# Warm-up matmuls of TensorE 512 columns wide in place of 128, in an RMS norm and QKV projection

## Chip, cores, metric

One core of a Trainium2 chip. The metric is the device time of one execution in microseconds. A run's time is some 1.8 us longer than the span of its profile, which goes from the first instruction to the last. Engines: PE is TensorE's matmul side, PEld its weight loads, DVE is VectorE, ACT is ScalarE, POOL is GpSimd, SP is SyncE, which here issues nearly all DMAs, strictly in program order.

## The reference

```python
batch, n_heads, seq, head_dim = 8, 12, 1024, 64      # dim = 768
rms = np.sqrt(np.mean(x ** 2, axis=-1, keepdims=True) + eps)
x_norm = x / rms * gamma
return np.matmul(x_norm, w_qkv)                       # 8192 x 768 times 768 x 2304, f32
```

## The kernel before

x is 64 tiles of 128 rows. Each tile is cast to bf16, transposed (tiles 0 to 2 by fp32 transposes on PE, tile 3 by bf16 ones, from tile 4 on by DMA, the helper `xbar`), multiplied with the bf16 weights into PSUM, scaled by 1/rms on the way out and stored. Gamma is folded into the weights when they are converted. The first 44 us, the head, follow a hand-made plan, in which weights arrive in 12 pieces. PE is kept busy with matmuls of zeros from the start, so that its clock is fast when data comes.

```python
warm = singles.tile([P, P], bf16)                 # P = 128, NT = 512
nc.vector.memset(warm, 0.0)
# ... (cut)
def idle(n):
    wps = psum.tile([P, P], f32, name="pm")
    for _ in range(n):
        nc.tensor.matmul(out=wps, lhsT=warm, rhs=warm, start=True, stop=True)
# ... (cut)
at(0.0, idle, 18)
at(2.8, gamma_in)                                 # one small transpose and a copy
at(2.81, idle, 28)
# ... (cut; the plan of the head has idle(3) at 7.26)
for t in range(HEAD, MT):                         # HEAD = 6, MT = 64
    ahead = 6.0 if t < HEAD + 5 else 0.0          # tiles 6 to 10 are prepared 6 us earlier
    if ("x", t) not in {q[1:] for q in LOADS}:
        at(now - 15 - ahead, load_x, t)
    at(now - 8.5 - ahead, cast, t)
    at(now - 7.5 - ahead, xbar, t)
    # ... (cut: statistics, 5 x 6 matmuls, evictions, stores)
```

## Time and profile before

| | before |
|---|---|
| time, median of 3 runs | 389.1 us (388.9 to 389.16) |
| span | 387.3 us |
| PE busy | 99% of the span |
| bytes moved by DMA | 119.91 MB, 310 GB/s on average |

PE is busy by this table from end to end. What it does not say is what PE waits for in the few places where it waits. The prediction shows those lines.

### The profile page before, as it was taken

How to read it: one execution, taken by the hardware profiler on the slowest of the kernel's cores; microseconds unless marked ns; L12 is line 12 of the kernel's file. 1: busy time of each engine (PE TensorE's matmuls, PEld its weight loads, DVE VectorE, ACT ScalarE, POOL GpSimd, SP SyncE). 2: the span in 40 equal slices, each digit the busy share in tenths (PEclk: the TensorE clock that was granted, in tenths of full speed). 3: DMA queues.
4: the chain of work that ended last, by engine and by line, in shares of the span. 5: the costliest groups of instructions: out<-in, count | busy, mean ns of one | idle time of the engine just before them, and what ended most of it. 6: DMA issues, size and time to landing. Idle time of an engine off the chain costs nothing.

```text
span 387.3 us, 5554 instructions
## 1 busy us (share of the span) xinstructions
PE 381.7 (99%) x1994; PEld 194.7 (50%) x1994; DVE 153.9 (40%) x309; ACT 181.2 (47%) x362; POOL 7.5 (2%) x15
## 2 busy tenths in 40 slices
PE   8999999999999999999999999999999999999996
PEld 7444654554554554554554554554554554554552
DVE  3565524444333344333344333343333343333332
ACT  5662444443544444544444444544444534444532
POOL 0312000000000000000000000000000000000000
PEclk9999999999999999999999999999999999999999
DMA  8999999999999999999999999999999999999974
GB/s 287 390 273 389 330 361 353 372 365 323 306 289 303 311 298 317 300 297 319 292 303 303 290 328 300 296 314 292 303 274 327 322 313 287 278 352 284 307 253 182
DMA packets 89511, 119.91 MB, mean 310 GB/s; under 512 B 52358, under 2 KB 61324, under 8 KB 89484
## 3 DMA queue, kind: packets, MB, share of 16 engines
q1 hardware_dynamic: 89472, 119.56, 101.1%
q8 instruction: 15, 0.25, 0.3%
q14 instruction: 12, 0.10, 0.1%
q10 hardware_dynamic: 12, 0.00, 0.0%
HBM read 32.25 MB, written 75.50 MB: 278 GB/s over the span
## 4 chain that ended last, share of the span: by engine, by line
PE 94%; DMA 4%; POOL 0%; SPq 0%; ACT 0%; issue 0%
PE pm L229 94%; DMA w_f<-in_w_qkv_dram 3%; DMA x_t<-in_x_dram 1%; POOL w_b L168 0%; ACT ot L245 0%; SPq L158 0%; SPq L153 0%
## 5 line engine op out<-in xcount | busy, mean ns | idle before, releaser
L229 PE MATMUL pm<-w_b,xT 128*128 128x512 bf16 (+1 forms) x1920 | 374.1, 358 | 0.5 <-DVE w_b L164 0.4
L229 PEld LDWEIGHTS <-xT 128*128 128x128 bf16 x1920 | 187.7, 98 | 186.4 <-issue 1.3
L243 DVE TENSOR_SCALAR ot<-pm,rstd 128x512 f32<-128x512 f32 (+1 forms) x165 | 113.6, 693 | 201.8 <-PE pm L229 201.5
L245 ACT ACTIVATE ot<-pm,rstd 128x512 f32<-128x512 f32 (+1 forms) x155 | 100.2, 647 | 191.5 <-PE pm L229 146.6
L183 ACT ACTIVATE sq<-x_t 128x768 bf16<-128x768 f32 x64 | 53.4, 835 | 1.3 <-DMA x_t<-in_x_dram 1.2
L172 DVE CAST xb<-x_t 128x768 bf16<-128x768 f32 x61 | 33.3, 546 | 16.7 <-DMA x_t<-in_x_dram 16.7
L185 ACT ACTIVATE rms<-ssq,eps_sb 128x1 f32<-128x1 f32 x64 | 18.9, 295 | 2.1
L183 ACT ACTIVATION_READ_ACCUMULATOR sq<-x_t 128x1 f32 x64 | 12.3, 192 | 0.0
L190 DVE RECIPROCAL rstd<-rms 128x1 f32<-128x1 f32 x64 | 9.8, 154 | 3.1 <-ACT rms L185 3.1
L166 ACT ACTIVATE w_b<-w_f,g_sb 128x512 bf16<-128x512 f32 (+1 forms) x9 | 5.8, 668 | 6.1 <-DMA w_f<-in_w_qkv_dram 6.1
L168 POOL TENSOR_SCALAR w_b<-w_f,g_sb 128x512 bf16<-128x512 f32 (+1 forms) x9 | 6.8, 764 | 24.1 <-DMA w_f<-in_w_qkv_dram 24.1
L164 DVE TENSOR_SCALAR w_b<-w_f,g_sb 128x512 bf16<-128x512 f32 (+1 forms) x12 | 5.2, 450 | 4.5 <-DMA w_f<-in_w_qkv_dram 4.4
L278 PE MATMUL pm<-warm 128*128 128x128 bf16 x49 | 5.2, 294 | 1.0 <-DVE eps_sb L137 1.0
L278 PEld LDWEIGHTS <-warm 128*128 128x128 bf16 x49 | 4.7, 138 | 1.0 <-DVE eps_sb L137 1.0
L210 PE MATMUL pm<-ident_f,x_t 128*128 128x128 f32 x18 | 2.5, 278 | 0.3 <-DMA x_t<-in_x_dram 0.3
L210 PEld LDWEIGHTS pm<-ident_f,x_t 128*128 128x128 f32 x18 | 1.9, 141 | 0.7 <-PE pm L278 0.5
L172 DVE CAST xT<-pm 128x512 bf16<-128x512 f32 (+1 forms) x3 | 1.8, 592 | 0.8 <-PE pm L210 0.8
L140 ACT ACT_TABLE_LOAD x1 | 1.3, 1283 | 1.3 <-PEq L334 1.3
L174 ACT CAST xT<-pm 128x256 bf16<-128x256 f32 (+1 forms) x3 | 1.2, 445 | 0.3 <-PE pm L210 0.2
L174 ACT COPY xT<-pm 128x768 bf16<-128x768 bf16 x1 | 0.8, 798 | 0.2 <-PE pm L196 0.2
L261 DVE COPY g_sb<-pm 128x6 f32<-128x6 f32 x1 | 0.2, 164 | 1.8 <-PE pm L260 1.8
L196 PEld LDWEIGHTS <-xb 128*128 128x128 bf16 x6 | 0.4, 98 | 0.2
(13 smaller groups left out, 2.4 us busy)
## 6 DMA issues: line engine op xcount, KB each, us to landing
out_dram<-ot SPq DMA_DIRECT2D x124, 512.0 KB, 3.9
x_t<-in_x_dram SPq DMA_DIRECT2D x64, 384.0 KB, 4.3
out_dram<-ot SPq DMA_DIRECT2D x64, 128.0 KB, 3.2
w_f<-in_w_qkv_dram SPq DMA_DIRECT2D x7, 768.0 KB, 8.1
out_dram<-ot SPq DMA_DIRECT2D x8, 256.0 KB, 2.0
w_f<-in_w_qkv_dram SPq DMA_DIRECT2D x4, 256.0 KB, 6.1
xT<-xb SPq DMA_TRANSPOSE x60, 4.4
w_f<-in_w_qkv_dram SPq DMA_DIRECT2D x1, 512.0 KB, 3.9
```

The costliest lines, as they stand in the source:

```text
L164: nc.vector.tensor_scalar(out=o, in0=i, scalar1=g, scalar2=None, op0=mult)
L166: nc.scalar.activation(out=o, in_=i, func=AF.Copy, scale=g, bias=0.0)
L168: nc.gpsimd.tensor_scalar(out=o, in0=i, scalar1=g, scalar2=1.0, op0=mult, op1=mult)
L172: nc.vector.tensor_copy(out=out, in_=in_)
L183: nc.scalar.activation(out=sq, in_=X[t], func=AF.Square, accum_out=ssq)
L185: nc.scalar.activation(out=rms, in_=ssq, func=AF.Sqrt, scale=inv_k, bias=eps_sb)
L190: nc.vector.reciprocal(out=r, in_=RS[t])
L210: nc.tensor.transpose(out=PT[t, h][:, ko - k0, :], in_=X[t][:, ko * P:(ko + 1) * P], identity=ident_f)
L229: nc.tensor.matmul(out=PM[t, n0][:, :nl], lhsT=XT[t][:, ko, :], rhs=w_b[:, ko, n0:n0 + nl], start=(b == 1), stop=(b == KO))
L243: nc.vector.tensor_scalar(out=o, in0=pm[:, :nl], scalar1=RS[t], scalar2=None, op0=mult)
L245: nc.scalar.activation(out=o, in_=pm[:, :nl], func=AF.Copy, scale=RS[t], bias=0.0)
L278: nc.tensor.matmul(out=wps, lhsT=warm, rhs=warm, start=True, stop=True)
```

## The change

Its intent is the same warm-up time with a fourth of the instructions: one matmul of 512 columns for four of 128.

```diff
-    warm = singles.tile([P, P], bf16)
+    warm = singles.tile([P, NT], bf16)
...
-    def idle(n):
-        wps = psum.tile([P, P], f32, name="pm")
+    def idle(n, nl=P):
+        wps = psum.tile([P, NT], f32, name="pm")
         for _ in range(n):
-            nc.tensor.matmul(out=wps, lhsT=warm, rhs=warm, start=True, stop=True)
+            nc.tensor.matmul(out=wps[:, :nl], lhsT=warm[:, :P], rhs=warm[:, :nl], start=True, stop=True)
...
-    at(0.0, idle, 18)
+    at(0.0, idle, 4, NT)
     at(2.8, gamma_in)
-    at(2.81, idle, 28)
+    at(2.81, idle, 6, NT)
+    at(2.82, idle, 3)
```

## The prediction

> **What bounds the kernel now.** I read four views in this order: the chain of work that ended last, TensorE's (PE's) row of waits, PE's timeline over the first 22 us, and the instructions of the warm-up line.
>
> The chain of the kernel before, in order of time (start us, length us, what):
>
> ```profile
> 1.75 4.86 DMA x_t<-in_x_dram
> ...
> 6.62 10.19 DMA w_f<-in_w_qkv_dram
> ...
> 16.90 0.99 POOL w_b L168
> ...
> 17.94 365.63 PE pm L229 x1883
> ...
> 383.59 0.47 ACT ot L245
> ```
>
> The end is set by three things in a row: input transfers until 16.82 us, one weight conversion on POOL, and then 365.63 us in which PE runs without a hole. The warm-up line (L278 of the kernel before) is nowhere in it. The last part is at the array's pace: the head's twelve 512-wide matmuls from 8.70 us span 2.75 us with a last one of 379 ns, so 11 intervals of 215.6 ns; the 1883 of the chain are 1499 of 512 columns (64 tiles x 24 = 1536, less the 37 issued before 17.94 us) and 384 of 256 columns. 1499 x 0.2156 + 384 x about 0.109 (my estimate: half, plus a little) = 365.0 us, against 365.63. Nothing is left to win there, and the warm-up, over by 8 us, cannot act there unless it leaves the array at a slow clock.
>
> PE's own waits over the whole kernel (who waited, for whom, us in total, times, longest):
>
> ```profile
> PE pm L278 <- DVE eps_sb L137: 1.0, 1, 1.0
> PE pm L229 <- DVE w_b L164: 0.4, 1, 0.4
> PE pm L210 <- DMA x_t<-in_x_dram: 0.3, 1, 0.3
> PE pm L229 <- POOL w_b L168: 0.2, 1, 0.2
> ```
>
> After the start, PE stands idle three times only: 0.33 us at 8.02 (third x tile), 0.36 at 17.38 and 0.18 at 17.94 (converted weights). All three are waits for input data. So if PE were earlier in the head it would stand there longer; if it were later by less than about 0.3 us before 8 us, or by less than 0.36 + 0.18 = 0.54 us after that, the holes would absorb it.
>
> PE's timeline over the head (start us, us, engine, line, operation, count):
>
> ```profile
> 0.99 2.10 PE L278 MATMUL pm<-warm 128*128 128x128 bf16 x18 [0.99 <-DVE eps_sb L137]
> 3.02 0.27 PE L260 MATMUL pm<-ident_f,g 6*128 6x6 f32 x1
> 3.22 2.79 PE L278 MATMUL pm<-warm 128*128 128x128 bf16 x28
> 5.84 1.68 PE L210 MATMUL pm<-ident_f,x_t 128*128 128x128 f32 x12
> ```
>
> And the warm-up line's own durations (min/median/max ns), then the numbers of its matmuls in stretches of 0.2 us (the first bracket of each stretch: PE busy, count):
>
> ```profile
> L278 PE MATMUL pm<-warm x49: 219/314/315, 1.0 to 7.5; 128*128 128x128 bf16 x49
> L133 DVE MEMSET warm<- x1: 112/112/112, 0.8 to 0.8; 128x64 uint32 x1
> ...
> 5.20:5.40 0.20, 0.20 (x5) 0.20 (x3) 1.00 0.95 384
> 5.40:5.60 0.20, 0.20 (x6) 0.20 (x4) 1.00 1.11 415
> 5.60:5.80 0.20, 0.20 (x8) 0.20 (x5) 1.00 1.11 338
> ```
>
> The reader should see the array become fast here: two kinds of duration (314 and 219 ns), and the counts rising from 5 to 8 in a stretch. The first 18 started over 0.99 + 2.10 - 0.315 - 0.99 = 1.785 us, 17 intervals of 105 ns. The 28 started over 2.79 - 0.219 = 2.57 us, 27 intervals. With 105 ns slow and 55.6 ns fast (skill, below), 105a + 55.6(27 - a) = 2570 gives a = 21.6, so the switch came at 3.22 + 21.6 x 0.105 = 5.5 us. The column of the granted clock says 1.00 throughout: it does not show this switch.
>
> **What the Trainium skill says.** (1) "TensorE: Matmul & The Clock Gate", section "What's actually happening": the array starts at half clock and goes to full after a busy window of about 3.4 us; "The HW doesn't count instructions", the windows run free of the kernel's start, so what counts is time spent busy. The trace agrees with a switch inside the busy time, 4.5 us after the first warm-up matmul; a single trace cannot show where the windows lie. (2) Same page, section "Wait — 56ns, not 53.3ns?": start to start is 106.7 / 426.7 ns at 128 / 512 columns while cold, 55.6 / 215.7 ns when warm. The trace has 105 and 215.6; the cold 512-wide case it does not have. So four cold 128-wide matmuls last as long as one of 512, and the array is busy to the same degree: no hole opens either way. (3) "VectorE: DVE Perf Modes", section "Zero memsets can be issued as uint32 (trn2)": one cycle per element, after halving. The 128-column tile shows as 64 uint32 elements in 112 ns; 512 columns make 256 elements.
>
> **The change part by part.**
> - Memset of the warm-up tile: 192 more elements. At one cycle each and 0.96 GHz (the VectorE clock on the skill's opening page "Trainium Kernel Development and Optimization", section "NeuronCore Architecture") I estimate 192 / 0.96 = +200 ns, so 112 becomes about 312 ns. The warm-up starts at about 1.19 us in place of 0.99. The memset of eps behind it moves to about 1.15 us; its user on ACT runs at 2.63, behind a table load, and the identity cast on DVE waits for POOL until 1.34. Neither moves.
> - First group: 18 x 105 = 1.89 us becomes 4 x 420 = 1.68 us. Its columns end at 1.19 + 1.68 = 2.87 us against 0.99 + 1.89 = 2.88. The gamma transpose keeps its 3.02 us, and the copy of gamma at 3.33 stays far ahead of its first use at 4.74.
> - Second group: starts at 3.22. With the switch again at 5.5 us, 2.28 us of cold time hold 5.43 of the six wide ones; the rest takes 0.57 x 0.216 = 0.12, and the three narrow ones 3 x 0.056 = 0.17. It ends at 5.79 us, against 5.79 + 0.056 = 5.85 for the 28. Difference: -0.06 us, in front of transposes of x.
> - The last three warm-up matmuls, at 7.36 us, stay as they are.
> - PSUM: the extra call of the helper allocates one more buffer of the ring of eight. It stands early; all later tiles keep their distance of eight to each other, and the few that now follow another owner follow one that is done before 6 us. Cost 0.
> - Instructions: 18 + 28 + 3 = 49 matmuls become 4 + 6 + 3 + 3 = 16, 33 fewer, and 33 fewer weight loads. They run beside nothing that waits for an instruction: cost or gain 0 on the path.
>
> Sum before 6 us: +0.20 - 0.21 - 0.06, some -0.06 us at the transposes. The second group of transposes then waits for its x tile (0.22 us on the weight-load row now) that much longer. On the path that sets the end: 0.00 us.
>
> **The rivals.**
> 1. A better warm-up: wide matmuls, with fewer weight loads between them, make the array count as busier, and the fast clock comes a window earlier. For it: the window is only seen through its result. Against it: the narrow ones already stream without a hole at 105 ns, and whatever PE wins before 8 us it loses waiting at 8.02, 17.38 and 17.94 us, for transfers that no warm-up releases. Time: 389.1, unchanged. Even no warm-up at all might cost little.
> 2. A worse one: start 0.2 us later, so that a window is not full and the switch comes one window (3.4 us by the skill) later, at about 8.9 us. Then 18 transposes of x run cold. They are started 100 ns apart now (six loads of weights span 0.64 us, the last of 141 ns: 0.50 / 5); at twice that they cost +1.8 us, of which some 0.33 + 0.54 are absorbed: about +0.9 us, 390.0. A second window missed would add about eight cold 512-wide matmuls at +0.21, another 1.7 us: 391.7. Against it: the busy time from 1.19 to 5.8 us is 4.6 us against 4.8 before, hardly less. I give it 7 in 100.
> 3. The longer memset delays the start and nothing gives it back (+0.2 us at the transposes). It fits in the hole at 8.02. Time: 389.1.
> 4. The transfers' order or pace changes because of the timing of PE. Against it: the queue issues inputs from 0.74 us on its own, and the first waits in it on an engine are for DVE (casts and evictions). Some tenths either way at most.
>
> **Range and chances.** The working gives 0.0 us on the time, so the median before: 389.1. Its three runs spread over 0.26 us; I take that on both sides, and a little more above for rival 2 in its mild form: 388.7 to 389.7. Within 2% means 381.3 to 396.9; a gain of 7.8 us would have to come out of the 365 us at the array's pace, or out of the transfers, and a loss of that size needs some 36 us of matmuls at half clock. Chances: faster 0.01, within 0.98, slower 0.01.
>
> **What would show it right or wrong.** Right: the chain after has PE L229 from about 17.94 us for about 365.6 us; the memset takes 0.3 us; the first warm-up group begins near 1.2 us and gamma's transpose stays near 3.0; the cold 512-wide rows read about 314 + (420 - 105) = 630 ns; the transposes of x start by 5.85 us. Wrong: L278 or the transposes in the chain; holes of PE at 8.02, 17.38 and 17.94 us all gone; or L229 matmuls after 8.7 us that start about 430 ns apart, which would be the switch come late. A start of the long PE stretch more than 0.3 us away from 17.94 would mean that the transfers moved after all.

## The result, and the profile after

The changed kernel took 389.43 us (median of 6 runs, 389.02 to 389.97) against 389.12 (388.9 to 389.19): ratio 1.0011, interval 0.9998 to 1.0023, the same within 2%. The time is in the predicted range. But three of the six runs lie at 389.0 to 389.2 and three at 389.7 to 390.0. The kernel before had no such second group in these six runs. It is not free of such runs, though: of its 18 runs in the rounds of the two repeats below, three lie above 389.5 (389.55, 389.63 and 390.02).

The warm-up itself went as worked out, but for the clock. PE's timeline of the changed kernel (start us, us, engine, line, operation, count), then the durations of the warm-up matmuls (min/median/max ns) and the memset:

```profile
1.19 1.89 PE L278 MATMUL pm<-warm 128*128 128x512 bf16 x4 [1.19 <-DVE eps_sb L137]
3.01 0.27 PE L260 MATMUL pm<-ident_f,g 6*128 6x6 f32 x1
3.21 3.06 PE L278 MATMUL pm<-warm 128*128 128x512 bf16 x9
6.06 1.78 PE L210 MATMUL pm<-ident_f,x_t 128*128 128x128 f32 x12
...
L278 PE MATMUL pm<-warm x16: 219/622/634, 1.2 to 7.8; 128*128 128x512 bf16 x10, 128*128 128x128 bf16 x6
L133 DVE MEMSET warm<- x1: 272/272/272, 0.9 to 0.9; 128x256 uint32 x1
```

The start is at 1.19, gamma's transpose at 3.01. The second group lasts 3.06 us, so its columns end 3.06 - 0.16 (the tail of the last one) = 2.90 us after its start, where I had worked out 2.57. All of it at the slow clock makes 6 x 0.420 + 3 x 0.105 = 2.84: no switch came inside the group, and it came later than in the profile before. (The trace's single records say the same: the group's nine matmuls take 607 to 634 ns or, the narrow ones, 314 ns, and of x's transposes behind them the first three take 421, 421 and 368 ns and the fourth 273, so the clock switched at about 6.5 us.)

PE's waits and its long stretches in the changed kernel:

```profile
PE pm L229 <- DMA xT<-xb: 1.0, 2, 0.7
...
23.36 50.55 PE L229 MATMUL pm<-w_b,xT 128*128 128x512 bf16 x262 [0.74 <-DMA xT<-xb]
74.16 309.43 PE L229 MATMUL pm<-w_b,xT 128*128 128x512 bf16 x1558 [0.25 <-DMA xT<-xb]
```

and the same of the kernel before, from the same view:

```profile
21.82 361.73 PE L229 MATMUL pm<-w_b,xT 128*128 128x512 bf16 x1865
```

The reader should see two things. First, the holes before converted weights at 17.4 and 17.9 us are gone, and a hole of 0.74 us at 23.36 us stands in their place: PE waits there for tile 4, transposed by DMA. What was gained before it is given back, as the prediction said it would be, only at another transfer. Second, there is a hole at 74.16 us, in the part which I had called one stretch without holes. It stands before tile 11. In the idle column it has 0.25 us. That counts from the modelled end of the last matmul, which runs 379 - 216 = 163 ns past the next possible start, so PE lost 0.41 us there. (38 of the 1920 L229 records are missing from this trace, so its counts and busy sums are a little low.)

SP's timeline shows where that tile comes from. Its issue of the transposes of tiles 8 and 11, with the load of an x tile and three stores in front of the first, in the kernel before:

```profile
43.42 0.45 SPq L153 DMA_DIRECT2D x_t<-in_x_dram  x1
43.96 2.33 SPq L249 DMA_DIRECT2D out_dram<-ot  x3
46.52 2.87 SPq L219 DMA_TRANSPOSE xT<-xb  x1
...
68.23 1.95 SPq L219 DMA_TRANSPOSE xT<-xb  x1
```

and in the changed kernel:

```profile
44.31 1.17 SPq L153 DMA_DIRECT2D x_t<-in_x_dram  x1
45.58 3.38 SPq L249 DMA_DIRECT2D out_dram<-ot  x3
49.04 2.31 SPq L219 DMA_TRANSPOSE xT<-xb  x1
...
69.32 1.75 SPq L219 DMA_TRANSPOSE xT<-xb  x1
```

Tile 8's transpose is issued 2.5 us later and tile 11's 1.1 us later. The order of SP's DMAs is the same in both traces; only their times differ. SP is late already before tile 8's transpose: by 0.9 us at the x load and by 1.6 us at the first of the three stores. Tile 8's own data are not what is late: its cast on DVE starts at 43.45 us, against 44.63 in the kernel before. Tile 11 is the first tile without the `ahead` of 6 us in the code above, so it has the least lead of all. PE is then at the mercy of when it lands.

So with a change in the first 6 us, the issue of DMAs at 46 and 68 us moved. The experiments ask whether that is where the time goes, and how it comes about.

### The profile page after: what moved, and what is told of

Same layout as the page of the kernel before. It is cut to its first block, busy times and chain, and to the rows that moved or that the text cites. A ratio compares the mean times of both kernels' runs of the same rounds, so it can differ in the third digit from the quotient of the medians.

```text
span 387.4 us, 5450 instructions
## 1 busy us (share of the span) xinstructions
PE 379.5 (98%) x1923; PEld 192.1 (50%) x1961; DVE 153.9 (40%) x309; ACT 181.2 (47%) x362; POOL 7.5 (2%) x15
## 4 chain that ended last, share of the span: by engine, by line
PE 91%; DMA 7%; issue 1%; SPq 0%; ACT 0%
PE pm L229 91%; DMA x_t<-in_x_dram 4%; DMA xT<-xb 3%; SPq L153 0%; ACT sq L183 0%; ACT ot L245 0%; SPq L158 0%
## 5 line engine op out<-in xcount | busy, mean ns | idle before, releaser
L229 PE MATMUL pm<-w_b,xT 128*128 128x512 bf16 (+1 forms) x1882 | 371.9, 357 | 2.9 <-DMA xT<-xb 1.0
L229 PEld LDWEIGHTS <-xT 128*128 128x128 bf16 x1920 | 187.5, 98 | 186.8 <-DMA xT<-xb 1.6
L172 DVE CAST xb<-x_t 128x768 bf16<-128x768 f32 x61 | 33.2, 544 | 20.4 <-DMA x_t<-in_x_dram 20.4
L278 PE MATMUL pm<-warm 128*128 128x512 bf16 (+1 forms) x16 | 5.3, 493 | 1.2 <-DVE eps_sb L137 1.2
L278 PEld LDWEIGHTS <-warm 128*128 128x128 bf16 x16 | 1.8, 131 | 3.4 <-issue 2.2
```

Source lines behind the costliest of these rows:

```text
L172: nc.vector.tensor_copy(out=out, in_=in_)
L229: nc.tensor.matmul(out=PM[t, n0][:, :nl], lhsT=XT[t][:, ko, :], rhs=w_b[:, ko, n0:n0 + nl], start=(b == 1), stop=(b == KO))
L278: nc.tensor.matmul(out=wps[:, :nl], lhsT=warm[:, :P], rhs=warm[:, :nl], start=True, stop=True)
```

## The experiments

Three theories were on the table. A: input transfers set the end, and the warm-up is off the path. B: what splits the runs is the clock, whose switch comes late in some executions. C: the spread is the wait at tile 11. A fourth, D, was formed after the eighth run: it is the number of instructions, through the DMAs that fetch them.

### The kernel before, again

No edit.

> The kernel before, unchanged, so that it is known how far two runs of one program differ here. Theory A (input transfers set the end, the warm-up is off the path): 389.1 us within 0.2, no run above 389.5, ratio 1.000. Theory B (the windows of the clock gate run free of the kernel, and the late switch costs some 0.7 us in some executions of any version): a part of these runs also lies near 389.8. The profile will show the time of the switch; under both theories it may differ from 5.5 us.

Measured: 388.95 us (388.81 to 389.38), ratio 0.9997. Its warm-up shows another switch time. The second group of 28 lasted 2.79 us in the first profile, here:

```profile
3.22 3.03 PE L278 MATMUL pm<-warm 128*128 128x128 bf16 x28
```

28 at the slow 105 ns throughout would be 27 x 0.105 + 0.219 = 3.05: here the switch came only at the group's end (its last three matmuls take 274, 223 and 219 ns), near 5.95 us. The time was 0.2 us lower all the same. Against B. None of these five runs lies above 389.5, as A expected; but two of the nine other runs of this kernel in the same rounds do (389.55 and 389.63), which A did not allow and B did.

### The changed kernel, again, twice

No edit.

> The changed kernel, unchanged. Its six runs fell in two groups, 389.02 to 389.16 and 389.70 to 389.97. Theory A: chance among other causes; 389.1 to 389.3 us, with at most one run in five above 389.5. Theory B1 (the change makes the costly late switch more frequent, since warm-up starts 0.2 us later and leaves less margin): two or more of five above 389.5, ratio about 1.001.

> The changed kernel once more, on the same chip as the run with the semaphore increments. Means of its runs so far 389.48 (six) and 389.63 (five). Theory D: 389.4 to 389.6, first packet at 20.5 us, tile 8's transpose near 49 us, a wait at tile 11 in most executions. If it is at 389.1, the difference between the two kernels was chance.

Measured: 389.45 us (389.0 to 390.45), ratio 1.0012 (0.9998 to 1.0025); and 389.75 us (389.42 to 389.85), ratio 1.0015 (1.0002 to 1.0027). The means of the changed kernel's runs less those of the kernel before in the same rounds are 0.42, 0.49 and 0.58 us in the three sets (389.48 and 389.06; 389.63 and 389.14; 389.70 and 389.12). Two of the first five runs lie above 389.5, which was B1's forecast and not A's. The mean of the last five is 0.1 us above D's 389.4 to 389.6. The difference between the kernels is small, but chance is an unlikely cause: over all three sets it is 0.48 us with a standard error of 0.12. One reading alone left it open.

The same two places in the profile of the first of these, a run of 390.45 us; then, for the other, a run of 389.75 us, its second warm-up group and PE's restart at tile 11 (the view was cut at 76 us):

```profile
23.52 50.55 PE L229 MATMUL pm<-w_b,xT 128*128 128x512 bf16 x262 [0.46 <-DMA xT<-xb]
75.44 309.43 PE L229 MATMUL pm<-w_b,xT 128*128 128x512 bf16 x1558 [1.37 <-DMA xT<-xb]
```

```profile
3.21 2.10 PE L278 MATMUL pm<-warm 128*128 128x512 bf16 x9
...
74.83 1.47 PE L229 MATMUL pm<-w_b,xT 128*128 128x512 bf16 x5 [0.46 <-DMA xT<-xb]
```

From tile 11 on PE needs 309.43 us in both of the whole stretches shown, to the last digit. So the end is the start of tile 11 plus a constant, and the hole before it goes into the time one for one. The lost times (idle + 0.16) are 0.41, 1.53 and 0.62 us; spans less these are 387.0, 387.1 and 387.3, about the spans of the kernel before (387.3 and 387.1). The wait does not go by the issue alone: the longest, 1.37 us idle, stands behind the earliest issue of tile 11's transpose of the three (68.95 us), so the time from issue to arrival varied as well. The profile of 389.75 us also settles B: its second group lasted 2.10 us, so the clock was fast there earlier than in either profile of the kernel before, and the run was still slow.

### The longer memset alone

```diff
-    warm = singles.tile([P, P], bf16)
+    warm = singles.tile([P, NT], bf16)
-            nc.tensor.matmul(out=wps, lhsT=warm, rhs=warm, start=True, stop=True)
+            nc.tensor.matmul(out=wps, lhsT=warm[:, :P], rhs=warm[:, :P], start=True, stop=True)
```

(in the kernel before)

> The warm-up tile is 512 wide and set whole, but the matmuls stay 128 wide and 18 + 28: the part of the change that delays the start by 0.2 us, alone. Theory A: 389.1 within 0.2. Theory B1 (a later start leaves less margin): some runs near 389.8, as with the change. Theory B2 (wide matmuls are what makes the switch late): all runs near 389.1.

Measured: 389.25 us (388.71 to 389.56), ratio 1.0000. Its warm-up begins at 1.19 us as in the changed kernel; no wait at tile 11. The later start costs nothing that can be seen, as A expected and against B1.

### No warm-up at all

```diff
-    at(0.0, idle, 18)
-    at(2.81, idle, 28)
```

(in the kernel before, and without the three at 7.26)

> No warm-up matmuls at all. Theory A with a little slack: the transposes of x start at about 5.7 us cold[...], 7 to 15 matmuls of 512 columns cost 0.21 us more each, 1.5 to 3.2 us in all, of which 0.5 to 0.9 are absorbed in holes: 389.8 to 391.5 us. If the time is within 0.3 us of 389.1, the whole warm-up is of no use; if it is above 392, the head depends on the clock far more than theory A allows.

Measured: 390.27 us (389.32 to 390.41), mean 390.03 against 389.14, ratio 1.0022 (1.0010 to 1.0035). PE's timeline:

```profile
5.53 4.34 PE L210 MATMUL pm<-ident_f,x_t 128*128 128x128 f32 x18 [3.03 <-DMA x_t<-in_x_dram]
9.66 3.64 PE L229 MATMUL pm<-w_b,xT 128*128 128x512 bf16 x12
```

The 12 matmuls span 3.64 us in place of 2.75, and the transposes are slow throughout. The time is in the expected range. All the warm-up is worth 0.9 us, 0.2% of the time (with the effect of its number of instructions, which this run does not separate), so there is little in it.

### More lead for the late tiles, in both kernels

```diff
-        ahead = 6.0 if t < HEAD + 5 else 0.0
+        ahead = 6.0
```

> The changed kernel with x loads, casts and transposes issued 6 us earlier for all tiles, where it was so up to tile 10 only. In the three traces over 388 us or of the changed kernel, TensorE stood 0.4 to 1.5 us before tile 11 (at 74 to 75 us), the first tile without the 6 us, for a transpose by DMA that was issued at 69 us; in the three traces of the narrow warm-up that transpose was issued at 68.2 to 68.4 us and there was no wait. Theory C (the spread of the changed kernel comes from that wait): the wait at tile 11 is gone, all runs lie within 0.4 us of each other and near 388.8 to 389.1. Theory B (late switch of the clock): the spread and the runs near 389.8 stay.

> The same edit of the transposes' lead in the kernel before. Theory C: same time as after_ahead within 0.2 us, 388.8 to 389.1, so that the warm-up's width is worth nothing once tile 11 can't be late. If the two still differ by 0.4 us as the unedited kernels do (means of all runs 389.1 and 389.5), theory C is wrong.

Measured: changed kernel 389.11 us (388.47 to 389.41), mean 388.98; kernel before 388.92 us (388.81 to 389.15), mean 388.95. Both have ratio 0.9994 (0.9981 to 1.0008) to the kernel before; one of the two has five timed runs, the other four. In the edited changed kernel tile 8's transpose still comes late, tile 11's comes early:

```profile
49.46 2.29 SPq L219 DMA_TRANSPOSE xT<-xb  x1
...
64.90 1.95 SPq L219 DMA_TRANSPOSE xT<-xb  x1
```

and PE has no wait there. The difference of 0.4 to 0.6 us between the kernels is gone (0.03, with a standard error near 0.2). Theory C stands: the wait at tile 11 is where the time went, as far as one profiled run of each kernel can tell. The spread did not fall as much as expected in the changed kernel (0.94 us between its runs, not 0.4). These are also the versions with the lowest means, but by 0.2 us, which is not clear of noise.

### Half of the change

```diff
-    at(0.0, idle, 4, NT)
+    at(0.0, idle, 18)        # on a 128-wide tile of its own; the wide tile is set behind eps
```

(in the changed kernel)

> Half of the change: first group 18 matmuls of 128 columns as before, on a tile of its own, second group 6 of 512 and 3 of 128; the start is at 1.0 us again, the wide tile is set later, behind the small one. Theory C with chance order in the transfers: 389.0 to 389.5; the tile 11 wait present where the transpose of tile 8 was issued near 49 us, absent where near 46.6 us. A theory by which wide matmuls in front of x's transposes themselves bring the other order: the trace has the tile 8 transpose near 49 us and the mean is near 389.5. A theory by which the later start does: as the kernel before, 389.1.

Measured: 389.63 us (389.33 to 389.80), mean 389.62, ratio 1.0012 (0.9999 to 1.0024). The start is at 1.0 us again, tile 8's transpose at 48.65, tile 11's at 69.69, and PE idle 0.89 us before tile 11. (The profile puts that wait to ACT's line 185, the statistics, which a matmul does not read; so what ended it is not told.) So the start is not it. By this run it could be the wide matmuls in front of x's transposes, as the expectation said, or their number: this kernel has 19 matmuls and 19 weight loads, so 38 instructions of PE, fewer than the kernel before.

### Four more matmuls at 12.6 us

```diff
+    at(12.63, late, 4)       # 4 x 512 columns of zeros into the buffer that the next matmul overwrites
```

(in the changed kernel)

> The changed kernel with four more 512-wide matmuls of zeros (4 x 0.216 = 0.86 us) at about 12.6 us, on the fast clock, into a buffer that the next matmul overwrites. Theory A: the wait for tile 4's transposed x (0.74 us in the trace) shrinks by what it can give; TensorE is late by 0.86 - 0.74 = about 0.1 us, plus up to 0.2 that lay unseen behind the last matmul: 389.0 to 389.7. If TensorE's pace from 12 us on set the end without slack, 390.3.

Measured: 389.95 us (389.62 to 392.03), mean 390.38, ratio 1.0034 (1.0014 to 1.0055). In the profiled run, of 389.72 us, the wait for tile 4 is nearly gone (0.05 us from start to start of the weight loads, against 0.90 in the changed kernel: 0.27 and 1.12 less 0.216). So 0.86 us of work were absorbed there as expected, and tile 11 still waited (0.51 us idle). The expectation of 389.0 to 389.7 was too low: one run lies in it, three more within 0.32 us above it, and 390.99 and 392.03 far above. Those two were not profiled; what they waited for is open.

### Theory D: whose DMAs are at 14.6 us?

The traces of all runs so far, but for the one without warm-up, fall into two groups by the times of SP's issues, not by the clock. What goes with the groups is one kind of packet: 16 KB each, 15 in a run, on queue q8, of the kind that the profile calls "instruction". (Queue q14 has a dozen packets of that kind too, of 8 KB.) Packets and bytes of that queue between 14.4 and 15.8 us in the kernel before, then between 20.4 and 21.8 us in the changed one:

```profile
q8 instruction: 1, 0.02, 4.9%
```

```profile
q8 instruction: 1, 0.02, 4.8%
```

The other kernel has none in either window. From the trace's records of single packets, the first three start at 14.62, 39.85 and 61.19 us before, and at 20.55, 46.03 and 67.88 us after; each takes about 1.1 us. The Trainium skill, "Runtime: NRT & Kernel Launch", section "Instruction fetch mechanics", says that each engine's instructions are refilled by DMA in 16 KiB blocks of 256 instructions, and that crossing a boundary is "mostly hidden". The traces agree with the blocks: 66 instructions fewer at the start, and each later block is wanted 66 instructions, some 6 us, later. From the fourth packet to the last of the kernel before they are 24.7 us apart on average; PE's 60 matmuls and weight loads for each tile of 5.83 us make 256 instructions in 24.9 us. The later packets then fall on other transfers: at 46 us in place of 40, at 68 in place of 61. Two runs cross the count with the width. They ran on another chip (15, the other experiments on 6), with the kernel before in their rounds (mean 389.04), but without the changed kernel.

**Wide, with the old count.**

```diff
-    at(2.81, idle, 6, NT)
+    at(2.805, tiny, 36)      # 36 matmuls of 1 column, weights of 1 column
+    at(2.81, idle, 3, NT)
```

(in the changed kernel)

> The changed kernel with the instruction count of the kernel before: 3 of the 6 wide matmuls of the second group give way to 36 matmuls of 1 column with weights of 1 column, so 33 pairs more. Theory D: the instructions of TensorE are fetched by DMA in packets of 16 KB; with 66 instructions fewer each packet comes some 6 us later (first at 20.5 us in place of 14.6), so that it falls on other transfers, above all on those of tile 8 and tile 11. Under D the first packet is back at 14.5 to 15 us, the tile 8 transpose is issued near 46.6 us, tile 11 waits for nothing, and the runs lie like those of the kernel before: mean 389.0 to 389.3. If it is the width of the matmuls, and not their number, the trace has the first packet or the tile 8 transpose where the changed kernel has it (20.5, 49 us), and the mean is near 389.5.

**Narrow, with the new count.**

```diff
-    at(0.0, idle, 18)
-    at(2.81, idle, 28)
+    at(2.81, idle, 13)
```

(in the kernel before)

> The kernel before with 33 warm-up matmuls fewer and no wide ones: no first group, 13 narrow ones in the second. Theory D: first packet of instructions at 20 to 21 us, tile 8's transpose near 49 us, a wait at tile 11, mean 389.4 to 390.3 (the clock switches later too, which costs part of it, as in the run without warm-up). If the width matters and not the number: first packet at 14.6 us, tile 8's transpose near 46.5 us and no wait at tile 11, whatever the clock does.

Measured. The wide one with the old count: first packet at 14.53 us, and in SP's timeline:

```profile
46.48 2.85 SPq L219 DMA_TRANSPOSE xT<-xb  x1
...
68.36 1.86 SPq L219 DMA_TRANSPOSE xT<-xb  x1
```

No wait at tile 11. The narrow one with the new count: first packet at 20.48 us, and:

```profile
48.74 2.21 SPq L219 DMA_TRANSPOSE xT<-xb  x1
...
68.83 2.36 SPq L219 DMA_TRANSPOSE xT<-xb  x1
```

Both go with the count and against the width, in the times of the issues. The prediction of a wait for the narrow one failed in its profile: PE did not wait at tile 11 there.

The times don't settle it as neatly. They are 389.39 us (388.92 to 391.16), mean 389.62, ratio 1.0018 (1.0002 to 1.0033), and 389.70 us (388.79 to 391.89), mean 389.84, ratio 1.0020 (0.9999 to 1.0040). The expected mean for the first was 389.0 to 389.3: missed. So the two kernels lie 0.58 and 0.80 us above the kernel before of their rounds (standard errors 0.35 and 0.47): by the times, the old count did not help the wide one. Both upset the clock, too. The 36 small matmuls took 1.04 us, and the transposes behind them ran slow: 12 of them span 2.52 us against 1.68 before. Two of the first one's runs, the profiled one among them, are at 388.9.

**The old count without touching the array.**

```diff
     at(0.0, idle, 4, NT)
+    at(0.1, count, 33)       # increments of a semaphore nobody waits for, on PE's stream
...
     at(2.81, idle, 6, NT)
+    at(2.815, count, 33)
```

(in the changed kernel)

> The changed kernel with all its matmuls, and 66 increments of a semaphore that nobody waits for put in TensorE's stream behind the wide matmuls, where the array is busy: the instruction count of the kernel before, without a change to the array's work or its clock. Theory D (the place of the instruction packets decides): first packet at 14.5 to 15 us, tile 8's transpose near 46.5 us, no wait at tile 11, and, unlike the run with the 36 small matmuls, which also upset the clock, a mean of 389.0 to 389.25 us, below the changed kernel of the same rounds by 0.2 to 0.5. If packets and order come back to those of the kernel before but the mean stays near 389.5, the order of transfers is caused by the packets and the time is not.

Measured: 394.91 us (394.54 to 396.46), ratio 1.0156 (1.0134 to 1.0177). A failed design. I had taken the increments for nearly free behind a busy array. PE's timeline:

```profile
6.35 0.24 PE L260 MATMUL pm<-ident_f,g 6*128 6x6 f32 x1 [3.27 <-issue]
...
11.37 0.48 PE L278 MATMUL pm<-warm 128*128 128x128 bf16 x3 [2.11 <-issue]
```

Gamma's transpose is at 6.35 us in place of 3.01 and the narrow matmuls at 11.37, so that all came some 5.7 us late and the packets with it (first at 20.52). As a test of D it failed: no packet came at 14.5 us. Measured against its own late head, the packets (20.5, 45.6 and 67.2 us) are where they are in the kernel before, tile 8's transpose follows tile 7's by 8.6 us (9.2 to 9.7 in the five profiles with the old count, 10.5 to 12.4 in the seven with fewer), and PE does not wait at tile 11. That agrees with D, but so late a head is no clean test. It does tell that a head late by 5.7 us is paid in full (394.91 - 389.09 = 5.8): the slack of the head is some tenths, not microseconds.

### All profiles side by side

First instruction packet, issue of the transposes of tiles 8 and 11 (us), PE's idle time before tile 11 (us, from the profile), and the mean time of all runs (us):

| kernel | packet | tile 8 | tile 11 | idle before tile 11 | mean |
|---|---|---|---|---|---|
| before | 14.6 | 46.5 | 68.2 | 0 | 389.06 |
| before, again | 14.8 | 46.7 | 68.4 | 0 | 389.02 |
| longer memset alone | 14.6 | 46.7 | 68.4 | 0 | 389.16 |
| wide, old count | 14.5 | 46.5 | 68.4 | 0 | 389.62 |
| before, more lead | 14.6 | 46.5 | 64.9 | 0 | 388.95 |
| changed | 20.6 | 49.0 | 69.3 | 0.25 | 389.48 |
| changed, again | 20.7 | 49.1 | 69.0 | 1.37 | 389.63 |
| changed, third | 21.0 | 49.6 | 69.5 | 0.46 | 389.70 |
| half of the change | 18.6 | 48.7 | 69.7 | 0.89 | 389.62 |
| four matmuls more | 20.7 | 48.9 | 69.0 | 0.51 | 390.38 |
| narrow, new count | 20.5 | 48.7 | 68.8 | 0 | 389.84 |
| changed, more lead | 20.6 | 49.5 | 64.9 | 0 | 388.98 |
| no warm-up | 24.1 | 46.3 | 68.2 | 0.17 | 390.03 |

With the packet at 14.5 to 14.8 us tile 8 is at 46.5 to 46.7 in five of five; at 18.6 to 21.0 it is at 48.7 to 49.6 in seven of seven. The run without warm-up has its packets at 24.1, 48.9 and 73.3 us, outside both groups. (The two crossed runs, "wide, old count" and "narrow, new count", ran on chip 15. The run with semaphore increments is left out, since its whole head is 5.7 us late.)

The packet at 46 us is not the whole answer. The first of the three stores in front of tile 8's transpose is issued at 43.7 to 44.0 us in the first five and at 44.7 to 45.9 in the seven; in four of these seven the packet starts only after that store (in the changed kernel the store is at 45.58 us and the packet at 46.03). Nor is it enough that no packet comes at 40 us: the run without warm-up has none there either, and its tile 8 is at 46.3. What does go with a packet everywhere is the head: from the issue of x tile 4's load to the start of its cast it takes 9.76 to 9.95 us in the five with a packet at 14.5 to 14.8, and 8.72 to 9.11 in the eight others. PE's holes before converted weights at 17 to 20 us stand in the same five profiles alone. So inputs came earlier where the first packet came later; how that leads to SP's late issues from 43 us on stays open.

## Why the prediction was right, and where it was not

- **Nothing to win.** Right. PE from the head's end is at the array's pace, and what it won early it gave back at the next transfer: the holes at 17.4 and 17.9 us became one at 23.36. But these holes did not go because of PE: they go with the packet at 14.6 us, which the prediction did not know of.
- **The warm-up's own sums.** Memset about 312 ns: 272. (The estimate rested on one cycle per element at 0.96 GHz; measured, 192 more elements took 160 ns, 0.83 ns each in place of the 1.04 of the estimate; the measurement decides.) Start 1.19: 1.19. Gamma's transpose 3.02: 3.01. Cold wide rows about 630 ns: 634; they start 427 ns apart, as the page cited in the prediction has it, and the narrow ones 106.7 apart after a shorter first interval, so 420 and 105 were a little low. The end of the second group and the start of the transposes stood on a switch "again at 5.5 us", and that failed: the transposes began at 6.06, not by 5.85. In another execution of the same kernel the switch came earlier than 5.5, by over 1 us. It cost nothing to speak of.
- **Rival 2, a late switch.** Its mechanism exists and its size was right to some tenths (no warm-up at all: +0.9 us). It does not explain the changed kernel's runs, since one with an early switch was slow. In the range, "some 36 us of matmuls at half clock" for a loss of 7.8 us is a wrong sum: at 0.21 us each it takes 37 matmuls, which at 0.43 us apart last 16 us.
- **Instructions: "33 fewer, and 33 fewer weight loads. They run beside nothing that waits for an instruction: cost or gain 0 on the path."** This is the step that failed, in its reason at the least. No instruction is seen to be waited for, but instructions are fetched by DMA beside x, weights and results, the fetch moved by 6 us, and with a packet in flight x tile 4 took 1 us longer. The time of tile 8's issue went with the count in twelve of twelve profiles. That the count alone costs the 0.4 to 0.6 us is not shown.
- **Rival 4, the order or pace of transfers changes.** It was named, for another reason (PE's timing), and dismissed with "some tenths either way at most". The pace did change (the order of SP's issues did not), and the size was right: +0.42 to +0.58 us on the mean, 0.1%.
- **"365 us without a hole."** Right for that trace, and too strong as a statement on the kernel: tile 11, the first without extra lead, was a near miss. A single trace cannot show how near.

The range held in part by luck. The median, 389.43 us, lies in the margin that was added for a late switch of the clock, and what used it up was something else; two of the six runs lie above the range's top of 389.7.

What is shown: the extra time lies in the wait at tile 11 (it goes into the end one for one, and more lead removes the difference), and the late issue of the transposes of tiles 8 and 11 goes with the number of instructions and not with the width of the matmuls (one profile of each crossed kernel). What is not shown: the chain of steps from the moved packets to SP's late issues from 43 us on; why the same late issue makes PE wait 0 us at tile 11 in one profile and 1.37 in another; and a run with the old count, an undisturbed clock and a time back at 389.1.

## What to carry to other kernels

A kernel that keeps PE and the DMA engines both full has its slack in single transfers: look for the tile with the least lead (here the first behind a change of the schedule) before judging what a change in another place will do. Here a change in the number of PE's instructions moved all later fetches of its instructions, so compare two versions by where their 16 KB instruction packets fall as well. A difference of 0.1% needed three sets of five runs or so, and more than one profile of each kernel.

## What the Trainium skill lacked or had wrong

- "Runtime: NRT & Kernel Launch", section "Instruction fetch mechanics": right on the blocks of 16 KiB. It calls a crossing "mostly hidden" and has nothing on the fetches competing with the kernel's own DMAs; here a packet takes about 1.1 us, x tile 4 took 1 us longer to its cast where a packet fell at 14.5 to 14.8 us, and with 66 instructions fewer a DMA issue at 46 us came 2.5 us later.
- "DMA: Bandwidth & Descriptors", section "Queues, rings and completion order", puts the refill on queue row 14; if the profile's queue numbers are these rows, the trace differs for PE: the 16 KB packets that follow its instruction count are on q8, 15 in a run, and q14 has a dozen instruction packets of 8 KB.
- "TensorE: Matmul & The Clock Gate", section "Single matmul latency": the cold form (219 + N) / 1.2 gives 289 ns at 128 columns and 609 at 512; the traces have 314 and 634 (25 ns more). The warm form gives 219 and 379, as in the traces. (The ends of matmuls are modelled in these profiles, so this compares two descriptions rather than the array itself.)
- The same page, section "What's actually happening": agrees. Windows that run free of the kernel fit a second warm-up group of 2.10 us in one execution and 3.06 us in two others of one program; the windows themselves no run shows.
- No page that I read has the cost of semaphore increments as instructions of their own in PE's stream: 33 of them behind the first group moved gamma's transpose from 3.01 to 6.35 us, at most (6.35 - 1.19) / 33 = 156 ns each.
